# Two-layer hybrid decoder on one core: first operands, memory rows, row maxima and last output rearranged

## The chip, the core and the metric

The kernel runs on one core of one Trainium2 chip. The metric is device time in microseconds of one execution. A core has a matrix engine (TensorE, PE in the profile; its weight loads are listed as PEld), a vector engine (DVE), a scalar engine (ACT), GpSimd (POOL), and SyncE (SP), which here only issues transfers. Each engine works through its own instructions in order, and semaphores tie them together.

## What is computed

A residual stream of 256 rows by 1024 columns goes through two layers and a last normalisation. Cut to what matters here:

```python
def hybrid_layer(x, mem, ...):
    h = rms_norm(x, g_mix)
    z = h @ w_in                      # q, k, v of 6 + 6 heads, q of 4 heads, 3 gate blocks
    gates = sigmoid(z[..., o3:])
    o_a = dilated_mixer(...)          # 6 heads, masked softmax, three groups mixed
    o_b = moba_attn(...)              # 6 heads, causal softmax
    o_m = memory_attn(q_m, rms_norm(mem, g_mem), w_mkv)   # 4 heads on 256 memory rows
    y = gates[0] * (o_a @ w_pa) + gates[1] * (o_b @ w_pb) + gates[2] * (o_m @ w_pm)
    x = x + y @ w_o
    hm = rms_norm(x, g_mlp)
    return x + square(relu(hm @ w_up)) @ w_down

for l in range(2):
    x = hybrid_layer(x, mem, ...)
out = rms_norm(x, norm_final)
```

## The kernel before

Every product is made in two-part precision. A float32 matrix is split into a rounded part `hi` and the rest `lo`; a product is then hi·hi + hi·lo + lo·hi, three matmuls (`mm3`). The weights, 1 MB or 768 KB at a time (a *unit*), are brought in by SP into one of three `raw` buffers. ACT copies a rounded `whi` from it and DVE subtracts to get `wlo` (`split_to`, lines 139 and 140). Activations are transposed by PE, multiplied by the gain, and split the same way into `ax` (`split_gain`, lines 163 and 164).

A unit is used in two to four *groups*. The last loop of the kernel runs over the groups and sets the order on all engines: for group j come first the small matmuls hung on it (`pe`, `mid`), then the group's own products (`emit`), the work in `pre`, then `split_to(j + 3)`, the next transfers, the work in `post`, and last the copying out of the group's own sums. `whi` and `wlo` have five buffers, so the splits can run ahead of the products by some groups. PSUM has eight banks, given out in the order in which they were freed (`ps`, `pf`).

Groups 0 to 5 of layer 1 make one block of gates, in pieces of one and two k-tiles, while x and the weights arrive tile by tile. Ahead of them PE runs 15 transposes of the identity (`WARM`), which nobody reads. Both k-tiles of a pair are transposed into one PSUM bank, ACT then takes `hi` and DVE `lo` of one k-tile after the other (`first_pair`). Groups 6 to 17 make q, k and v of six heads. Their rotary part is done by DVE (lines 235, 236) and GpSimd (237, 238).

The memory rows are brought into a fourth use of the `raw` buffers at group 14, squared and summed by ACT at groups 17 and 18 (`mem_stats`, line 208), and their projection for k and v, `w_mkv`, is used in groups 24 to 27.

The scores of a head are made at the start of its group (`h_scores`). `h_max` (line 361) then adds the mask, takes the row maximum and frees the bank. It stands in `post`, behind the split of a later group's weights. Exponentials (391), sums and scaling (416), transposes (424) and the product with v follow in later groups.

At the end the last group adds 256 columns at a time to x for the second 128 rows, squares them on ACT, multiplies by the last gain, and scales by the power -0.5 of the mean square that GpSimd takes (`finish_out`). The output leaves in four transfers from SP.

Of the kernel before, what the change touches and what calls it, by code (L numbers as in the profile page):

```python
# [11 lines left out]
F32 = mybir.dt.float32  # L12
F32R = mybir.dt.float32r
BF16 = mybir.dt.bfloat16
AF = mybir.ActivationFunctionType
ALU = mybir.AluOpType
# [3 lines left out]
P = 128  # L20
D = 1024
S = 256
# [11 lines left out]
SHUF = list(range(8, 16)) + list(range(0, 8)) + list(range(16, 32))  # L34
QK_SCALE = HD ** -0.5
LOOK = 3
WARM = 15


@with_exitstack  # L40
def hybrid_kernel(ctx, tc, x, mem, memT, gains, g_final, rope, masks, w_in, w_pa, w_pb, w_pm,
                  w_out, w_mkv, w_up, w_down, out):
    nc = tc.nc
# [9 lines left out]
    def ps():  # L53
        b = free_banks.popleft()
        t = psp.tile([P, 512], F32, tag=f"b{b}", name=f"ps_b{b}", bufs=1)
        bank_of[id(t)] = (b, t)
        return t

    def pf(t):
        free_banks.append(bank_of.pop(id(t))[0])  # L60

    def sb(shape, dt, tag, bufs, shift=None):

        n = int(np.prod(shape[1:]))
# [27 lines left out]
    gain = sb([P, 3 * DEPTH, KT], F32, "gain", 1)  # L95
    xs = sb([P, 2, D], F32, "x", 1)
# [65 lines left out]
    def split_gain(hi, lo, src, g):  # L162
        nc.scalar.activation(hi, src, AF.Copy, scale=g)
        nc.vector.scalar_tensor_tensor(lo, src, g, f32(hi), op0=ALU.mult, op1=ALU.subtract)
# [40 lines left out]
    def square_sum(src, acc, keep=True):  # L205
        w = src.shape[1]
        junk = sb([P, 1024], BF16, "P", 5)[:, :w] if keep else src
        nc.scalar.activation(junk, src, AF.Square, accum_out=acc)
# [275 lines left out]
    def layer(l):  # L484
# [10 lines left out]
        for n in range(2):  # L495
            for br in range(3):
                col = OG + br * D + n * 512
                b = {}

                def emit(first, last, ks, br=br, n=n, b=b):  # L500
                    def f(hi, lo):
                        if first:
                            b["p"] = [ps() for _ in range(2)]
                        for t in range(2):
                            tt = slice(t * P, (t + 1) * P)
                            for c, k in enumerate(ks):
                                ah, al, _ = st["hT"][k // 4]
                                mm3(b["p"][t], ah[:, k % 4, tt], al[:, k % 4, tt], hi[:, c, :],
                                    lo[:, c, :], k == 0, k == KT - 1)
                        if last:  # L510
                            fn = AF.Copy if b["raw"] else AF.Sigmoid

                            def ev():
                                for t in range(2):
                                    nc.scalar.activation(
                                        gate(br, t, n), b["p"][t], fn,
                                        scale=1.0 if b["raw"] else st["rstd"][:, t:t + 1])
                                    pf(b["p"][t])
                            return ev
                    return f  # L520

                def block(emit=emit, col=col, cuts=((2, 2), (2, 2))):
                    for h, cut in enumerate(cuts):
                        k0 = 4 * h
                        ks = [k0 + sum(cut[:i]) for i in range(len(cut))]
                        unit([(win[:, k0:k0 + 4, col:col + 512], 4)], 4, 512, cut,
                             [emit(k == 0, k + c == KT, list(range(k, k + c)))
                              for k, c in zip(ks, cut)])
                b["raw"] = len(gate_units) < n_raw
                if b["raw"]:  # L530
                    raw_blocks.append((br, n))
                gate_units.append(block)
# [291 lines left out]
        add = lambda g, w, fn, i, *a: groups[g][w].append(lambda: fn(l, i, *a))  # L824
        for i in range(16):
            add(S0[i], "pe", h_scores, i)
            add(S0[i], "post", h_max, i)
            if i in (2, 5):
                add(S0[i] + 1, "post", h_exp, i - 2, i)
                d = 0 if l and i == 2 else 1  # L830
                add(S0[i] + 1 + d, "post", h_exp, i - 1, i)
                add(S0[i] + 2 + d, "post", h_exp, i, i)
                add(S0[i] + 3 + d, "pre", h_den, i)
                dens.update({ii: S0[i] + 3 + d for ii in range(i - 2, i + 1)})
            elif i >= 6:
                add(S0[i] + 1, "post", h_exp, i, i)
                add(S0[i] + 2, "pre", h_den, i)
                dens[i] = S0[i] + 2
# [75 lines left out]
    def finish_out(t, acc=None, r2=None):  # L914

        m0, o0 = fin[t]
        o1 = sb([P, 512], F32, "P", 5)
        r = sb([P, 1], F32, "fr", 2)
        pieces = [rs_state[DEPTH - 1, "next"][:, t, 1:2]]
        if acc is not None:  # L920
            s2 = sb([P, 2], F32, "ss2", 1)
            pieces = [s2[:, i:i + 1] for i in range(2)]
            for i in range(2):
                xx = xs[:, t, 512 + 256 * i:768 + 256 * i]
                nc.vector.scalar_tensor_tensor(xx, acc[t, 1][:, 256 * i:256 * i + 256],
                                               r2[:, t:t + 1], xx, op0=ALU.mult, op1=ALU.add)
                square_sum(xx, pieces[i])
        nc.vector.tensor_tensor(o1, xs[:, t, 512:], gfin[0][:, 512:], op=ALU.mult)
        for ss in pieces:
            ms = sb([P, 1], F32, "fm", 3)  # L930
            nc.vector.scalar_tensor_tensor(ms, ss, 1.0 / D, m0, op0=ALU.mult, op1=ALU.add)
            m0 = ms
        nc.gpsimd.tensor_tensor(r, ms, neghalf[:, 0:1], op=ALU.pow)
        if t == 0:
            nc.gpsimd.tensor_scalar(o1, o1, r, 1.0, op0=ALU.mult, op1=ALU.mult)
        else:
            nc.vector.tensor_scalar(o1, o1, r, None, op0=ALU.mult)
        nc.sync.dma_start(out[t * P:(t + 1) * P, 512:], o1)
        nc.scalar.activation(o0, o0, AF.Copy, scale=r)
        nc.sync.dma_start(out[t * P:(t + 1) * P, :512], o0)  # L940
# [2 lines left out]
    mem_state = {}  # L943

    def mem_rows_load():
        mem_state["m"] = sb([P, 2, D], F32, "raw", 3)
        nc.sync.dma_start(mem_state["m"], mem.rearrange("(t p) d -> p t d", p=P))

    def mem_stats(t):
        if t == 0:  # L950
            mem_state["ss"] = sb([P, 2], F32, "ss0", 2)
        square_sum(mem_state["m"][:, t, :], mem_state["ss"][:, t:t + 1], keep=False)
# [69 lines left out]
    first_ps = {}  # L1022

    def first_transpose(c):
        p = first_ps[c] = ps()
        for i in range(4):
            k, t = 2 * c + i // 2, i % 2
            nc.tensor.transpose(p[:, i * P:(i + 1) * P], xs[:, t, k * P:(k + 1) * P], ident)

    def first_operand(k):  # L1030
        hi, lo, _ = L[0]["hT"][k // 4]
        p = first_ps[k // 2]
        split_gain(hi[:, k % 4, :], lo[:, k % 4, :], p[:, k % 2 * S:(k % 2 + 1) * S],
                   gain[:, 0, k:k + 1])
        if k % 2:
            pf(p)

    def first_pair(c):
        first_transpose(c)
        first_operand(2 * c)  # L1040
        first_operand(2 * c + 1)


    busy = ps()
    for _ in range(WARM):
        nc.tensor.transpose(busy[:, :P], ident, ident)
    pf(busy)
    warm = sb([P, 2], F32, "warm", 1)
    nc.scalar.activation(warm, neghalf, AF.Exp)
    first_transpose(0)  # L1050
    for k in range(2):
        first_operand(k)
        split_to(k)

    def first_stats():
        ss = sb([P, 2], F32, "ss0", 2)
# [1 line left out]
            square_sum(xs[:, t, :], ss[:, t:t + 1])  # L1058
        L[0]["rstd"] = rstd_of(mean_square(ss, 1), "rstd")

    for c, j in ((1, 0), (2, 2), (3, 3)):
        groups[j]["pre"].append(lambda c=c: first_pair(c))
    groups[5]["pre"].append(first_stats)
    groups[8]["mid"] = lambda: row_tables(0, L[0]["rstd"])
    g1, gm = L[1]["g0"], [L[l]["g_mem"] for l in range(DEPTH)]
    groups[gm[0] - 10]["pre"].append(mem_rows_load)
    groups[gm[0] - 7]["post"].append(lambda: mem_stats(0))
    groups[gm[0] - 6]["post"].append(lambda: mem_stats(1))
    groups[gm[0] - 4]["pre"].append(mem_rstd)
    groups[gm[0] + 1]["mid"] = mem_rows  # L1070
    for l in range(DEPTH):
# [88 lines left out]
```

## Time and profile before

| | |
|---|---|
| runs, median (lowest to highest) | 770.65 us (770.24 to 771.03), 3 runs |
| the profiled execution | 771.88 us, its span 770.1 us |
| PE busy | 755.7 us |
| DVE busy | 569.1 us |
| ACT busy | 466.8 us |
| GpSimd busy | 73.9 us |
| read from memory | 137.52 MB, 180 GB/s over the span |

A row of the timeline gives start, duration, engine, line, operation, output <- inputs with their shapes, and in brackets how long the engine had stood idle before it and what released it. Consecutive matmuls overlap, so the time that one costs is the distance from its start to the next one's start, not its listed duration. In a row of waits the numbers are the total, how often, and the longest.

### The profile page before, as it was taken

What the parts mean: (1) busy time and instruction counts of PE and PEld (TensorE: products, weight loads), DVE (VectorE), ACT (ScalarE), POOL (GpSimd) and SP (SyncE); (2) the same over time, 40 slices, a digit from 0 to 9 for tenths busy, and PEclk for the clock granted to TensorE, in tenths of its full rate; (3) what the DMA queues carried; (4) which work ended last, traced back from release to release, by engine and by line L of the source; (5) the groups of instructions that cost most, each with busy time, mean ns of one, the idle gap of its engine ahead of it and who ended that gap; (6) DMA issues with size and microseconds to landing.
All of it is one profiled execution on the core that took longest, in us unless ns stands there. A gap on an engine that the chain in (4) does not pass through costs nothing.

```text
span 770.1 us, 11176 instructions
## 1 busy us (share of the span) xinstructions
PE 755.7 (98%) x4237; PEld 663.6 (86%) x4237; DVE 569.1 (74%) x969; ACT 466.8 (61%) x812; POOL 73.9 (10%) x79
## 2 busy tenths in 40 slices
PE   8999999999999999999999999999999999999996
PEld 6998899888888888898889899888888888888885
DVE  4799999849786655766568989986787766566654
ACT  4777878784565544655455777869546555445542
POOL 1342030003000000000003211300110000000000
PEclk9999999999999999999999999999999999999999
DMA  8847444544647558565536455453655655666441
GB/s 280 254 158 260 126 168 159 166 163 165 196 139 244 165 186 273 183 199 165 205 123 201 154 183 172 151 181 125 203 172 165 200 191 164 203 219 206 163 151 54
DMA packets 92197, 139.28 MB, mean 181 GB/s; under 512 B 2928, under 2 KB 53104, under 8 KB 92144
## 3 DMA queue, kind: packets, MB, share of 16 engines
q1 hardware_dynamic: 92000, 138.55, 54.7%
q8 instruction: 33, 0.54, 0.3%
q14 instruction: 20, 0.16, 0.1%
q10 hardware_dynamic: 144, 0.02, 0.0%
HBM read 137.52 MB, written 1.05 MB: 180 GB/s over the span
## 4 chain that ended last, share of the span: by engine, by line
PE 57%; issue 29%; DVE 7%; ACT 4%; POOL 2%; DMA 1%; POOLq 0%; ACTq 0%; DVEq 0%
PE ps_b L148 13%; PE ps_b L149 13%; PE ps_b L150 13%; PE ps_b L154 8%; PE ps_b L155 4%; DVE wlo L140 2%; PE ps_b L424 1%; ACT whi L139 1%; DVE qk L218 1%; PE ps_b L451 1%; POOL rs L237 1%; PE ps_b L344 1%; POOL rc L238 1%; PE ps_b L343 1%; PE ps_b L450 1%
## 5 line engine op out<-in xcount | busy, mean ns | idle before, releaser
L140 DVE TENSOR_TENSOR wlo<-raw,whi 128x1024 fp32r<-128x1024 f32 (+2 forms) x266 | 305.7, 1180 | 46.3 <-ACT whi L139 45.7
L139 ACT ACTIVATE whi<-raw 128x1024 fp32r<-128x1024 f32 (+2 forms) x266 | 260.2, 1008 | 28.5 <-PE ps_b L150 9.7
L154 PE MATMUL ps_b<-ax,whi 128*128 128x512 f32 x512 | 179.5, 391 | 0.0
L155 PE MATMUL ps_b<-ax,wlo 128*128 128x256 f32 x512 | 144.3, 282 | 0.0
L148 PE MATMUL ps_b<-whi,ax 128*128 128x512 f32 (+1 forms) x320 | 125.6, 393 | 1.8 <-ACT whi L139 1.8
L149 PE MATMUL ps_b<-wlo,ax 128*128 128x512 f32 (+1 forms) x320 | 122.1, 381 | 0.2 <-DVE wlo L140 0.2
L150 PE MATMUL ps_b<-whi,ax 128*128 128x512 f32 (+1 forms) x320 | 122.0, 381 | 0.0
L154 PEld LDWEIGHTS ps_b<-ax,whi 128*128 128x128 f32 x512 | 96.1, 188 | 20.6
L148 PE MATMUL ps_b<-whi,qk 128*128 128x512 f32 x256 | 99.8, 390 | 0.0
L149 PE MATMUL ps_b<-wlo,qk 128*128 128x512 f32 x256 | 99.8, 390 | 0.0
L150 PE MATMUL ps_b<-whi,qk 128*128 128x512 f32 x256 | 99.7, 389 | 0.0
L155 PEld LDWEIGHTS ps_b<-ax,wlo 128*128 128x128 f32 x512 | 96.7, 189 | 1.1
L703 ACT ACTIVATE P<-ps_b 128x256 f32<-128x256 f32 x64 | 24.1, 382 | 104.8 <-PE ps_b L155 104.8
L705 DVE TENSOR_TENSOR P<-ps_b,P 128x256 f32<-128x256 f32 x64 | 26.7, 423 | 76.1 <-ACT P L703 76.1
L148 PEld LDWEIGHTS ps_b<-whi,ax 128*128 128x128 f32 x320 | 60.4, 189 | 11.1 <-ACT whi L139 2.6
L150 PEld LDWEIGHTS ps_b<-whi,ax 128*128 128x128 f32 x320 | 60.3, 189 | 10.4
L149 PEld LDWEIGHTS ps_b<-wlo,ax 128*128 128x128 f32 x320 | 60.5, 189 | 9.6 <-DVE wlo L140 1.0
L148 PE MATMUL ps_b<-ax,whi 128*128 128x256 f32 x224 | 63.6, 284 | 0.0
L149 PE MATMUL ps_b<-ax,whi 128*128 128x256 f32 x224 | 62.7, 280 | 0.0
L150 PE MATMUL ps_b<-ax,wlo 128*128 128x256 f32 x224 | 62.7, 280 | 0.0
L148 PEld LDWEIGHTS ps_b<-whi,qk 128*128 128x128 f32 x256 | 48.1, 188 | 10.1
L150 PEld LDWEIGHTS ps_b<-whi,qk 128*128 128x128 f32 x256 | 48.1, 188 | 10.1
(150 smaller groups left out, 1076.4 us busy)
## 6 DMA issues: line engine op xcount, KB each, us to landing
raw<-in_w_up SPq DMA_DIRECT2D x32, 1024.0 KB, 5.9
raw<-in_w_down SPq DMA_DIRECT2D x32, 1024.0 KB, 4.9
raw<-in_w_in SPq DMA_DIRECT2D x24, 1024.0 KB, 5.1
raw<-in_w_in SPq DMA_DIRECT2D x24, 768.0 KB, 4.5
raw<-in_w_out SPq DMA_DIRECT2D x8, 1024.0 KB, 5.0
raw<-in_w_mkv SPq DMA_DIRECT2D x4, 1024.0 KB, 5.2
raw<-in_w_pm SPq DMA_DIRECT2D x4, 512.0 KB, 3.3
raw<-in_w_pb SPq DMA_DIRECT2D x4, 512.0 KB, 3.7
```

Of the source, the lines that this page charges most:

```text
L139: nc.scalar.activation(hi, src, AF.Copy)
L140: nc.vector.tensor_sub(lo, src, f32(hi))
L148: nc.tensor.matmul(o, lhsT=lh, rhs=rh, start=start, stop=False)
L149: nc.tensor.matmul(o, lhsT=lh, rhs=rl, start=False, stop=False)
L150: nc.tensor.matmul(o, lhsT=ll, rhs=rh, start=False, stop=stop)
L154: nc.tensor.matmul(o, lhsT=lh, rhs=rr, start=start, stop=False)
L155: nc.tensor.matmul(o[:, :S], lhsT=ll, rhs=rr[:, 0, :], start=False, stop=stop)
L218: nc.vector.tensor_sub(q[b, j, :], qf[a, :], f32(q[a, j, :]))
L237: nc.gpsimd.tensor_tensor(sh, sh, sinr, op=ALU.mult)
L238: nc.gpsimd.tensor_tensor(c, c, sh, op=ALU.add)
L703: nc.scalar.activation(tt[:, i, :], p[i][:, S:], AF.Copy)
L705: nc.vector.tensor_tensor(tt[:, i, :], p[i][:, :S], tt[:, i, :], op=ALU.add)
```

## The change

- **First operands.** The idle transposes are 12 ahead of the first pair of x tiles and 4 behind it, in place of 15 ahead. Each k-tile is transposed into a bank of its own. The first k-tile gets `hi` and `lo` both from DVE, and ACT begins with the first two splits of weights. The second pair is taken k-tile by k-tile, each followed by its split of weights. In groups of one k-tile the three terms run hi·hi, lo·hi, hi·lo, each over both row halves.
- **Memory rows.** They are loaded at group 8, in place of 14, into the buffer that later holds the gates (`gate12`), not into a `raw` buffer. Their squares move to groups 11 and 12.
- **Masks and row maxima.** `h_max` moves from `post` to `pre`, ahead of its group's `split_to`, for all 16 heads of both layers.
- **Last output.** For the second 128 rows the multiplication by the gain is cut in two, half of it behind the mean; the scaling is shared by ACT (256 columns) and DVE; ACT issues one of three transfers. The two squares share one scratch buffer.

```diff
-WARM = 15
+WARM = (12, 4)
...
+                    def f1(hi, lo):
...
+                        for a, w in ((ah, hi), (al, hi), (ah, lo)):
+                            for t in range(2):
+                                nc.tensor.matmul(b["p"][t], lhsT=a[:, k % 4, t * P:(t + 1) * P],
+                                                 rhs=w[:, 0, :], start=first and a is ah and w is hi,
+                                                 stop=False)
...
-            add(S0[i], "post", h_max, i)
+            add(S0[i], "pre", h_max, i)
...
+            junk = sb([P, 1024], BF16, "P", 5)
             for i in range(2):
...
-                square_sum(xx, pieces[i])
+                nc.scalar.activation(junk[:, 256 * i:256 * i + 256], xx, AF.Square,
+                                     accum_out=pieces[i])
+            m = sb([P, 1], F32, "fm", 3)
+            nc.vector.tensor_tensor(o1[:, :256], xs[:, t, 512:768], gfin[0][:, 512:768],
+                                    op=ALU.mult)
+            nc.vector.scalar_tensor_tensor(m, pieces[0], 1.0 / D, m0, op0=ALU.mult, op1=ALU.add)
+            ms = sb([P, 1], F32, "fm", 3)
+            nc.vector.scalar_tensor_tensor(ms, pieces[1], 1.0 / D, m, op0=ALU.mult, op1=ALU.add)
+            r = sb([P, 1], F32, "fr", 2)
+            nc.gpsimd.tensor_tensor(r, ms, neghalf[:, 0:1], op=ALU.pow)
+            nc.vector.tensor_tensor(o1[:, 256:], xs[:, t, 768:], gfin[0][:, 768:], op=ALU.mult)
+            nc.scalar.activation(o0[:, 256:], o0[:, 256:], AF.Copy, scale=r)
+            nc.scalar.dma_start(out[t * P:(t + 1) * P, 256:512], o0[:, 256:])
+            nc.vector.tensor_scalar(o1, o1, r, None, op0=ALU.mult)
+            nc.sync.dma_start(out[t * P:(t + 1) * P, 512:], o1)
+            nc.vector.tensor_scalar(o0[:, :256], o0[:, :256], r, None, op0=ALU.mult)
+            nc.sync.dma_start(out[t * P:(t + 1) * P, :256], o0[:, :256])
+            return
...
-        mem_state["m"] = sb([P, 2, D], F32, "raw", 3)
+        mem_state["m"] = sb([P, 4096], F32, "gate12", 1)[:, :2 * D].rearrange(
+            "p (t d) -> p t d", t=2)
...
-        p = first_ps[c] = ps()
-        for i in range(4):
-            k, t = 2 * c + i // 2, i % 2
-            nc.tensor.transpose(p[:, i * P:(i + 1) * P], xs[:, t, k * P:(k + 1) * P], ident)
+        for k in (2 * c, 2 * c + 1):
+            p = first_ps[k] = ps()
+            for t in range(2):
+                nc.tensor.transpose(p[:, t * P:(t + 1) * P], xs[:, t, k * P:(k + 1) * P], ident)
...
+            nc.vector.tensor_scalar(hi[:, 0, :], p[:, :S], g, None, op0=ALU.mult)
+            nc.vector.scalar_tensor_tensor(lo[:, 0, :], p[:, :S], g, f32(hi[:, 0, :]),
+                                           op0=ALU.mult, op1=ALU.subtract)
...
+    keep_busy(WARM[0])
...
     first_transpose(0)
-    for k in range(2):
-        first_operand(k)
-        split_to(k)
+    keep_busy(WARM[1])
+    pf(busy)
+    first_operand(0)
+    split_to(0)
+    split_to(1)
+    first_operand(1)
...
+    groups[0]["pre"].append(second_pair)
...
-    groups[gm[0] - 10]["pre"].append(mem_rows_load)
-    groups[gm[0] - 7]["post"].append(lambda: mem_stats(0))
-    groups[gm[0] - 6]["post"].append(lambda: mem_stats(1))
+    groups[gm[0] - 16]["pre"].append(mem_rows_load)
+    groups[gm[0] - 13]["post"].append(lambda: mem_stats(0))
+    groups[gm[0] - 12]["post"].append(lambda: mem_stats(1))
```

ACT at the start of the program, before the change. `ax` is the activation operand, `whi` the rounded weights, a number behind a name tells buffers apart:

```order
L1049 ACT_TABLE_LOAD
L1049 ACTIVATE warm<-neghalf 128x2
L163 ACTIVATE ax<-ps_b_131,gain 128x256
L139 ACTIVATE whi<-raw 128x512
L163 ACTIVATE ax<-ps_b_131,gain 128x256
L139 ACTIVATE whi<-raw 128x512
L163 ACTIVATE ax<-ps_b_156,gain 128x256 x2
L139 ACTIVATE whi<-raw 128x512 x2
```

The same place after the change:

```order
L1081 ACT_TABLE_LOAD
L1081 ACTIVATE warm_126<-neghalf_67 128x2
L139 ACTIVATE whi_140<-raw_92 128x512
L139 ACTIVATE whi_144<-raw_92 128x512
L163 ACTIVATE ax_111<-ps_b2_131,gain_88 128x256
L163 ACTIVATE ax_111<-ps_b5_158,gain_88 128x256
L139 ACTIVATE whi_166<-raw_92 128x512
L163 ACTIVATE ax_111<-ps_b6_161,gain_88 128x256
L139 ACTIVATE whi_172<-raw_92 128x512
```

Two splits of weights now stand ahead of the first operand that ACT takes, and every operand comes out of a bank of its own.

DVE at group 24, before the change, from the scaling of the first head's exponentials (416) to the copying out of the second rotary tile (235, 236); `ps_b7_863` are the scores of the fourth head:

```order
L416 TENSOR_SCALAR P_679<-P_679,rd_896 128x128
L416 TENSOR_SCALAR P_679<-P_679,rd_896 128x256
L140 TENSOR_TENSOR wlo_901<-raw_762,whi_900 128x1024
L361 ISA P_907,mxt_906<-ps_b7_863,mask_91 128x128
L361 ISA mxt_906 128x1
L361 ISA P_907,mxt_906<-ps_b7_863,mask_91 128x256
L361 ISA mxt_906 128x1
L235 TENSOR_TENSOR rc_910<-cosr_319,ps_b3_734 128x256
L236 STREAM_SHUFFLE rs_911<-ps_b3_734 128x256
```

The same place after the change:

```order
L361 ISA P_904,mxt_903<-ps_b5_868,mask_91 128x128
L361 ISA mxt_903 128x1
L361 ISA P_904,mxt_903<-ps_b5_868,mask_91 128x256
L361 ISA mxt_903 128x1
L416 TENSOR_SCALAR P_679<-P_679,rd_901 128x128
L416 TENSOR_SCALAR P_679<-P_679,rd_901 128x256
L140 TENSOR_TENSOR wlo_910<-raw_774,whi_909 128x1024
L235 TENSOR_TENSOR rc_915<-cosr_324,ps_b4_739 128x256
L236 STREAM_SHUFFLE rs_916<-ps_b4_739 128x256
```

The row maximum (361) has gone ahead of the scaling and of the split; the nine instructions are the same nine, and the rotary tile still ends the row.

## Rows read from the trace of the kernel before

**Rows 1.** Page, part 1: busy time, share of span, instructions per engine.

```profile
PE 755.7 (98%) x4237; PEld 663.6 (86%) x4237; DVE 569.1 (74%) x969; ACT 466.8 (61%) x812; POOL 73.9 (10%) x79
```

**Rows 2.** Waits of PE, whole span: total us, times, longest.

```profile
PE ps_b L424 <- DVE P L416: 1.4, 1, 1.4
...
PE ps_b L424 <- DVE mxt L361: 0.8, 1, 0.8
PE ps_b L150 <- DVE wlo L140: 0.7, 1, 0.7
```

**Rows 3.** Timeline, first 23 us: start, duration, engine, line, operation, idle before.

```profile
1.38 3.46 PE L1046 MATMUL ps_b<-ident 128*128 128x128 f32 x15 [1.38 <-POOL ident masks.py:199]
...
4.64 1.06 PE L1028 MATMUL ps_b<-ident,x 128*128 128x128 f32 x4
...
6.10 0.62 ACT L139 ACTIVATE whi<-raw 128x512 fp32r<-128x512 f32 x1
6.24 0.48 DVE L164 SCALAR_TENSOR_TENSOR ax<-ps_b,gain,ax 128x256 fp32r<-128x256 f32 x1 [6.24 <-ACT ax L163]
...
6.75 0.69 DVE L140 TENSOR_TENSOR wlo<-raw,whi 128x512 fp32r<-128x512 f32 x1
...
6.78 0.80 PE L148 MATMUL ps_b<-whi,ax 128*128 128x512 f32 x1 [1.08 <-ACT whi L139]
...
8.94 0.63 PE L149 MATMUL ps_b<-wlo,ax 128*128 128x512 f32 x1
...
9.37 0.63 PE L150 MATMUL ps_b<-whi,ax 128*128 128x512 f32 x1
...
12.77 0.49 PE L148 MATMUL ps_b<-whi,ax 128*128 128x512 f32 x1 [0.72 <-ACT whi L139]
...
22.53 0.28 PE L148 MATMUL ps_b<-ax,whi 128*128 128x256 f32 x1
```

**Rows 4.** Stretches: length, busy us of each engine, granted clock, DMA share, GB/s.

```profile
5.00:10.00 5.00, 3.92 (x11) 2.49 (x10) 2.20 (x4) 1.98 (x4) 0.00 (x0) 1.00 0.98 332
```

**Rows 5.** Transfers issued in the first 1.4 us: count, size, us to landing.

```profile
x<-in_x SPq DMA_DIRECT2D x1, 256.0 KB, 3.4
raw<-in_w_in SPq DMA_DIRECT2D x1, 256.0 KB, 3.5
```

**Rows 6.** Timeline of ACT, then of DVE, 30 to 75 us.

```profile
34.03 0.86 ACT L216 ACTIVATE qk<-rc 64x256 fp32r<-64x256 f32 x2 [1.68 <-POOL rc L238]
...
55.72 1.06 ACT L208 ACTIVATE raw<-raw 128x1024 f32<-128x1024 f32 x1
...
54.66 1.14 DVE L313 SCALAR_TENSOR_TENSOR Va<-ps_b,rstd,Va 128x384 fp32r<-128x384 f32 x2 [0.63 <-ACT Va L312]
...
58.02 0.96 DVE L140 TENSOR_TENSOR wlo<-raw,whi 128x768 fp32r<-128x768 f32 x1 [0.24 <-ACT whi L139]
...
73.30 0.43 DVE L236 STREAM_SHUFFLE rs<-ps_b 128x256 f32<-128x256 f32 x1
```

**Rows 7.** Timeline of DVE and PE in layer 2, at its first scores.

```profile
435.17 1.23 DVE L140 TENSOR_TENSOR wlo<-raw,whi 128x1024 fp32r<-128x1024 f32 x1 [0.28 <-ACT whi L139]
...
436.52 0.42 DVE L361 CUSTOM_DVE_ANT_0 P<-ps_b,mask 128x256 f32<-128x256 f32 x1
...
437.24 0.39 PE L148 MATMUL ps_b<-whi,ax 128*128 128x512 f32 x1
437.47 0.39 PE L149 MATMUL ps_b<-wlo,ax 128*128 128x512 f32 x1
```

**Rows 8.** Timeline of the end, from the last gain to the last transfer.

```profile
764.28 0.69 DVE L928 TENSOR_TENSOR P<-x,gate 128x512 f32<-128x512 f32 x1 [0.24 <-ACT P L208]
...
765.40 0.56 POOL L933 TENSOR_TENSOR fr<-fm,neghalf 128x1 f32<-128x1 f32 x1 [1.77 <-DVE fm L931]
765.99 0.72 ACT L939 ACTIVATE P<-P,fr 128x512 f32<-128x512 f32 x1 [1.35 <-POOL fr L933]
...
766.88 0.43 SPq L940 DMA_DIRECT2D out<-P  x1
```

More of the change, by code (lines that the diff above doesn't have):

```diff
@@ L500, in emit, with f0 @@
                 def emit(first, last, ks, br=br, n=n, b=b):
-                    def f(hi, lo):
+                    def f0(hi, lo):
                         if first:
@@ L509, in f, with f2 @@
                                     lo[:, c, :], k == 0, k == KT - 1)
+                    def f1(hi, lo):
+                        k = ks[0]
+                        if first:
+                            b["p"] = [ps() for _ in range(2)]
+                        ah, al, _ = st["hT"][k // 4]
+                        for a, w in ((ah, hi), (al, hi), (ah, lo)):
[3 more added lines that the diff above has]
+                                                 stop=False)
+                    def f2(hi, lo):
+                        f0(hi, lo)
                         if last:
@@ L519, in f @@
                             return ev
-                    return f
+                    return f1 if len(ks) == 1 else f2
                 def block(emit=emit, col=col, cuts=((2, 2), (2, 2))):
@@ L917, in finish_out @@
         o1 = sb([P, 512], F32, "P", 5)
-        r = sb([P, 1], F32, "fr", 2)
         pieces = [rs_state[DEPTH - 1, "next"][:, t, 1:2]]
@@ L926, in finish_out @@
                                                r2[:, t:t + 1], xx, op0=ALU.mult, op1=ALU.add)
-                square_sum(xx, pieces[i])
+                nc.scalar.activation(junk[:, 256 * i:256 * i + 256], xx, AF.Square,
[16 more added lines that the diff above has]
+            return
+        r = sb([P, 1], F32, "fr", 2)
         nc.vector.tensor_tensor(o1, xs[:, t, 512:], gfin[0][:, 512:], op=ALU.mult)
[L929 to L932, printed above, removed]
+        ms = sb([P, 1], F32, "fm", 3)
+        nc.vector.scalar_tensor_tensor(ms, pieces[0], 1.0 / D, m0, op0=ALU.mult, op1=ALU.add)
         nc.gpsimd.tensor_tensor(r, ms, neghalf[:, 0:1], op=ALU.pow)
[L934 to L937, printed above, removed]
+        nc.gpsimd.tensor_scalar(o1, o1, r, 1.0, op0=ALU.mult, op1=ALU.mult)
         nc.sync.dma_start(out[t * P:(t + 1) * P, 512:], o1)
@@ L1024, in first_transpose, with keep_busy @@
     def first_transpose(c):
-        p = first_ps[c] = ps()
-        for i in range(4):
-            k, t = 2 * c + i // 2, i % 2
-            nc.tensor.transpose(p[:, i * P:(i + 1) * P], xs[:, t, k * P:(k + 1) * P], ident)
+        for k in (2 * c, 2 * c + 1):
+            p = first_ps[k] = ps()
+            for t in range(2):
+                nc.tensor.transpose(p[:, t * P:(t + 1) * P], xs[:, t, k * P:(k + 1) * P], ident)
     def first_operand(k):
         hi, lo, _ = L[0]["hT"][k // 4]
[L1032 to L1041, printed above, removed]
+        p = first_ps[k]
+        if k:
+            split_gain(hi[:, k % 4, :], lo[:, k % 4, :], p[:, :S], gain[:, 0, k:k + 1])
+        else:
+            g = gain[:, 0, :1]
+            nc.vector.tensor_scalar(hi[:, 0, :], p[:, :S], g, None, op0=ALU.mult)
+            nc.vector.scalar_tensor_tensor(lo[:, 0, :], p[:, :S], g, f32(hi[:, 0, :]),
+                                           op0=ALU.mult, op1=ALU.subtract)
+        pf(p)
     busy = ps()
-    for _ in range(WARM):
-        nc.tensor.transpose(busy[:, :P], ident, ident)
-    pf(busy)
+    def keep_busy(count):
+        for _ in range(count):
+            nc.tensor.transpose(busy[:, :P], ident, ident)
+    keep_busy(WARM[0])
     warm = sb([P, 2], F32, "warm", 1)
@@ L1059, in first_stats, with second_pair, next_pair @@
         L[0]["rstd"] = rstd_of(mean_square(ss, 1), "rstd")
-    for c, j in ((1, 0), (2, 2), (3, 3)):
-        groups[j]["pre"].append(lambda c=c: first_pair(c))
+    def second_pair():
+        first_transpose(1)
+        for k in (2, 3):
+            first_operand(k)
+            split_to(k)
+    def next_pair(c):
+        first_transpose(c)
+        for k in (2 * c, 2 * c + 1):
+            first_operand(k)
+    groups[0]["pre"].append(second_pair)
+    for c, j in ((2, 2), (3, 3)):
+        groups[j]["pre"].append(lambda c=c: next_pair(c))
     groups[5]["pre"].append(first_stats)
```

## The prediction

> **What bounds the kernel now.** I read the page's busy shares first: PE is busy 755.7 us, 98% of the span [rows 1]. So almost everything is matmul time that this change leaves alone, and only three things can move the end: the stretches in which PE stands, the stretch in which it runs slowly, and what comes after its last product. Next I read the waits of PE [rows 2]. They are few: 0.7, 0.8 and 1.4 us, all on DVE and all between 60 and 90 us, in layer 1's attention. The third view is the timeline of the first 23 us [rows 3]. There PE stands 1.08 us ahead of its first real product at 6.78, and 0.72 us again at 12.77. It also runs slowly: products of 512 columns start 0.43 us apart at 8.94 and 9.37, the 1.2 GHz level, where later they start 0.23 apart, the 2.4 GHz level [rows 7]. The granted clock of 5 to 10 us is printed as 1.00 [rows 4]; the distances contradict it there, and I go by them. The same row shows the DMA engines 0.98 busy, so the first tiles arrive as fast as they can. The last view is the end: the chain from the last gain through GpSimd's power to the last output transfer [rows 8].
>
> **First operands.** Before, 15 idle transposes and then the pair's own four run from 1.38; the 15 take 4.64 - 1.38, or 0.217 us each [rows 3]. Twelve end at 3.99. The first x transfer lands 3.4 us after an issue inside the first microsecond [rows 5], so at about 4.1, and the pair starts at about 4.15. Four transposes are 0.87 us, to 5.02, and four more idle ones end at 5.89. Is the first product ready by then? From the start of a lone transpose to its reader is 1.06 us for four [rows 3], less three distances of 0.217, or 0.41. So DVE can begin on the first k-tile at 4.15 + 0.22 + 0.41 = 4.78. The new `hi` on DVE is an instruction that the trace of before does not show. Its nearest row is `lo` at 0.48 us on the same shape, which also reads a second tensor; I take 0.48, between a half of it and all of it. Then `hi` is there at 5.26, `lo` at 5.74, and `wlo` (0.69) at 6.43. ACT, whose first tile of weights lands at about 4.7 (3.5 us after an issue at about 1.2, [rows 5]), has `whi` (0.62) at 5.4. So all is ready and PE starts at 5.9 in place of 6.78.
>
> From there I count PE's own work up to the first product of the q block, which before starts at 22.53 [rows 3]. It is 48 products (six in each of four groups, twelve in each of two) at 0.227, or 10.9 us, and three sets of four transposes at about 0.35, together 11.9 us at the high clock. Now the clock. Before, PE was still slow at 9.37 [rows 3]; I put the rise right behind that, at 10.0, and take the same moment for the change. Work done between 5.9 and 10.0 runs at half speed, which costs 4.1 / 2 = 2.05 us. The end is 5.9 + 11.9 + 2.05 = 19.9, against 22.53: a gain of 2.6 us.
>
> This holds only if no operand is late. Before, ACT took its second `hi` of a pair only when DVE had read its `lo` of the first out of the same bank; with a bank for each k-tile it need not wait. Group 0 ends at 5.9 + 6 x 0.43 = 8.5, the second pair's transposes at 9.35, ACT has `hi` and `whi` of k-tile 2 at about 10.6, DVE its `wlo` at 11.3. PE comes to them at 11.1 and needs `wlo` only at its fifth product, at 12.0. So the wait of 0.72 goes, and what is next late is nothing up to the q block. If instead the old waits came back whole, 0.72 and about 0.5 behind it, the gain would be 1.4. If the clock rose before the first product, PE would be bound by the arriving weights. The last two tiles' splits then make the end about 18.3, a gain of 4.2. These are the ends, 1.4 and 4.2.
>
> Does the gain last? The weights' splits behind it run five groups ahead and wait for PE to free buffers, so they move with it; the transfers wait on the splits and have DMA time over. DVE's own chain starts from sums that PE gives it in the q block, so it moves too.
>
> **Memory rows.** ACT's two squares (1.06 us, [rows 6]) stand now in a stretch in which ACT has no pause. DVE waits behind them: 0.63 us for the copies of v and 0.24 us for a split [rows 6], some 0.9 together, and I add 0.3 for smaller pauses. At groups 11 and 12 ACT has pauses, 1.68 us in one row, while it waits for GpSimd's rotary part [rows 6], so there I cost the squares at nothing; without that cover each costs its 1.06 us on ACT, of which DVE would feel a part. The load at group 8 is queued on SP between two weight units and needs no free `raw` buffer, so nothing behind it waits for a buffer. It lengthens the next unit's landing by some 3 us (1 MB at the 332 GB/s of [rows 4]), which the run ahead of several groups hides. The `raw` buffer that it gives back lets the units of `w_mkv` start sooner.
>
> What does PE get from it? Its last wait, 1.4 us, ends when DVE has scaled the third head [rows 2]. Up to that instruction DVE has the same work as before, so PE's release moves by exactly the pauses that DVE loses: 1.2 us. The waits do not vanish. I expect some 1.9 of the 2.9 us to stay. The bounds are 0.3 (only the short pause goes) and 2.9 (all go).
>
> **Masks and row maxima.** The same instructions in another order: the 0.8 us wait at the first transposes of probabilities is for the bank that `h_max` frees [rows 2], and that now comes sooner. But right behind it PE needs the bank that the rotary copy at 73.30 frees [rows 6], and in both orders that comes after the same nine instructions. The wait moves by one instruction of PE and keeps its end, so the gain is nothing. The cost: what `h_max` is moved past, `wlo` of a group three further on, comes later by its 0.6 to 0.7 us (0.42 of it in [rows 7]). The tightest place I found is layer 2's first scores. There `wlo` ends at 436.40 and PE reads it at 437.47 [rows 7], 1.07 us of room; 0.28 of the addition falls into a pause of DVE. I take nothing. The bounds are a gain of 0.8 (the bank was the end) and a loss of 0.6 at each of the six earliest heads of the two layers, 3.6.
>
> **Last output.** Before, DVE's gain product of 0.69 us at 764.28 stands ahead of the mean, which waits for nothing else; GpSimd starts at 765.40 [rows 8]. Now half of it stands ahead and half behind, and GpSimd can start once the second square is in, at about 764.95: 0.45 us. Behind the power, ACT's scaling of 512 columns (0.72) ended ahead of the last issue at 766.88 [rows 8]; now 256 columns on DVE behind a scaling of 512 give the last issue at about 766.4, so 0.5 in all. The last piece is half as large, which gives up to 0.3 more. I take 0.7, between 0.3 and 0.9. On the second queue, the Trainium skill ("Trainium Kernel Development and Optimization", Key Constraints) says that queues of several engines share the same 16 DMA engines and save issue time alone. By that the term would be 0.5; no row of before has output on two queues.
>
> **Sum.** 2.6 + 1.2 + 0 + 0.7 = 4.5 us. The profiled execution took 771.88 us, a span of 770.1 and 1.8 around it; the sum makes that 767.4. The median of the runs, 770.65, is 1.2 lower than the profiled one, and I carry the gain over to it: 766.1.
>
> **The rivals.** *The clock rises sooner (0.28).* PE now never stands between 1.38 and the first products but for some 0.2 us, where it stood 1.08 us before. If the idle transposes keep the clock's count going, PE is at 2.4 GHz by the first groups, and the head gains 4.2: 770.65 - 4.2 - 1.2 - 0.7 = 764.5. Against it stands that the 19 transposes up to 4.64 + 1.06 = 5.7 left the products at 9.37 slow. The Trainium skill ("TensorE: Matmul & The Clock Gate", Part 4) says that transposes do not count as busy for the clock. By that this rival falls, and the forecast stands; the rows at 8.94 and 9.37 agree but cannot prove it, since PE also stood in between.
>
> *The head's gain is eaten (0.12).* DVE's pauses in this stretch are short [rows 6]. If it is the bound from its first split on, and its chain does not start sooner, PE reaches the same three waits 2.6 us earlier and waits that much longer: 770.65 - 1.2 - 0.7 = 768.7. Against it stands that DVE's chain begins with PE's sums.
>
> *The maxima hold up the splits (0.05), slower.* In `pre`, DVE waits for PE's scores ahead of each split. If the run ahead were lost at every head, each of 32 would cost 0.6 us or more: 19 us, less the 4.5, makes 785. It is slower than before from some 8 heads on. Only layer 1's first heads and those of [rows 7] have so little room.
>
> *Nothing moves (0.05)*: 770.6, where the transfers set the head after all, and DVE the rest.
>
> **How the numbers follow.** The forecast has 0.50, and its own range is 764.9 to 767.5 from the bounds of its terms. About 0.2% (1.5 us) is what a measurement of this kernel can tell from no change. Faster by more: the forecast, the sooner clock and most of the third case, 0.90; within it 0.06; slower 0.04. The range from 763.8 to 768.7 takes in the sooner clock and the eaten gain, and leaves out some 0.15.
>
> **What would show it.** Right: the first product at 5.9, no wait of PE between there and the q block, which starts near 19.9; the 1.08 and 0.72 gone; waits of PE between 60 and 90 us of 1.5 to 2.2 us, with the 0.7 on `wlo` gone; no squares on ACT near 52; the last power about 0.45 us closer to the last product. Wrong: products 0.23 apart before 8 us (the sooner clock), waits of PE in that stretch of 4 us or more (the eaten gain), or new waits on `wlo` at the groups of scores (the slower rival).

## The result and the profile after

The changed kernel takes 765.17 us (median of 5 runs, 764.85 to 765.66) against 770.65 us (770.24 to 772.18) for the kernel before: a ratio of 0.9925, 95% interval 0.9911 to 0.994. It is 5.5 us faster, where 4.5 was forecast. The profiled execution took 765.22 us, a span of 763.4. The span has lost 6.7 us, more than the median, because the profiled execution of before was 1.2 us above its own median; what those 1.2 us were turns out to matter below.

Part 1 of the page of the changed kernel, in the columns of [rows 1]:

```profile
PE 753.7 (99%) x4238; PEld 663.5 (87%) x4238; DVE 568.1 (74%) x972; ACT 465.1 (61%) x811; POOL 70.7 (9%) x79
```

Its waits of PE, in the columns of [rows 2]:

```profile
PE ps_b L1077 <- POOL ident masks.py:199: 1.4, 1, 1.4
PE ps_b L344 <- DVE kz L229: 0.9, 1, 0.9
PE ps_b L424 <- DVE P L416: 0.5, 1, 0.5
PE ps_b L1057 <- DMA x<-in_x: 0.2, 1, 0.2
```

The first line is the wait for the identity at the start, the second the one at layer 2's first scores. Neither is touched: the kernel before has both, at the same length, and the prediction's list of the waits left the second one out. Between 60 and 90 us 0.5 is left of the 0.7, 0.8 and 1.4 of [rows 2]. The forecast left 1.9.

The start of the timeline, to be held against [rows 3]:

```profile
1.38 2.82 PE L1077 MATMUL ps_b<-ident 128*128 128x128 f32 x12 [1.38 <-POOL ident masks.py:199]
4.37 1.12 PE L1057 MATMUL ps_b<-ident,x 128*128 128x128 f32 x4 [0.16 <-DMA x<-in_x]
5.09 0.48 DVE L1067 TENSOR_SCALAR ax<-ps_b,gain 128x256 fp32r<-128x256 f32 x1 [5.09 <-PE ps_b L1057]
5.27 1.06 PE L1077 MATMUL ps_b<-ident 128*128 128x128 f32 x4
5.99 1.75 PE L519 MATMUL ps_b<-whi,ax 128*128 128x512 f32 x4
7.57 0.63 PE L519 MATMUL ps_b<-wlo,ax 128*128 128x512 f32 x2
8.39 1.17 PE L519 MATMUL ps_b<-whi,ax 128*128 128x512 f32 x4
...
18.96 0.28 PE L148 MATMUL ps_b<-ax,whi 128*128 128x256 f32 x1
```

The first product starts at 5.99 (forecast 5.9), and the new `hi` on DVE costs the 0.48 us that the forecast took. But from 7.57 on two products start 0.23 us apart: PE is at its 2.4 GHz level by then, where the forecast put the rise at 10.0. The trace agrees: its records of the granted clock begin at 7.22 us, and in the kernel before at 10.33. Ahead of its first record a view prints 1.00, and so [rows 4] shows 1.00 for a stretch in which PE was slow. The q block starts at 18.96, 3.6 us sooner than in [rows 3], where 19.9 was forecast. That is the rival with the sooner clock. From there to the last product the changed kernel gains 2.9 us more, and behind it 0.2.

The end, to be held against [rows 8]:

```profile
756.68 0.88 DVE L940 SCALAR_TENSOR_TENSOR x<-ps_b,r,x 128x256 f32<-128x256 f32 x2 [0.96 <-PE ps_b L150]
758.27 0.42 DVE L952 TENSOR_TENSOR P<-x,gate 128x256 f32<-128x256 f32 x1
758.44 0.67 POOL L951 TENSOR_TENSOR fr<-fm,neghalf 128x1 f32<-128x1 f32 x1 [1.29 <-DVE fm L949]
759.14 0.51 ACT L953 ACTIVATE P<-P,fr 128x256 f32<-128x256 f32 x1 [0.98 <-POOL fr L951]
...
760.03 0.43 SPq L958 DMA_DIRECT2D out<-P  x1
```

From the last addition to x to the power it is 1.76 us, and before it was 765.40 - 763.16 = 2.24: the 0.48 forecast as 0.45. The rest of that term did not come (point 4 below).

### The profile page after: what moved, and what is told of

It is laid out like the page before. It is cut to its first block, busy times and chain, and to the rows that moved or that the text cites. A ratio compares the mean times of both kernels' runs of the same rounds, so it can differ in the third digit from the quotient of the medians.

```text
span 763.4 us, 11175 instructions
## 1 busy us (share of the span) xinstructions
PE 753.7 (99%) x4238; PEld 663.5 (87%) x4238; DVE 568.1 (74%) x972; ACT 465.1 (61%) x811; POOL 70.7 (9%) x79
## 4 chain that ended last, share of the span: by engine, by line
PE 56%; issue 30%; DVE 7%; DMA 2%; POOL 2%; ACT 2%; SPq 0%; POOLq 0%; DVEq 0%; ACTq 0%
PE ps_b L148 13%; PE ps_b L150 13%; PE ps_b L149 13%; PE ps_b L154 8%; PE ps_b L155 4%; DVE wlo L140 2%; DMA raw<-in_w_in 2%; PE ps_b L424 1%; DVE qk L218 1%; PE ps_b L451 1%; PE ps_b L344 1%; PE ps_b L343 1%; PE ps_b L450 1%; POOL rs L237 1%; POOL rc L238 1%
## 5 line engine op out<-in xcount | busy, mean ns | idle before, releaser
L148 PE MATMUL ps_b<-whi,ax 128*128 128x512 f32 (+1 forms) x312 | 121.6, 390 | 0.0
L150 PE MATMUL ps_b<-whi,ax 128*128 128x512 f32 (+1 forms) x312 | 118.4, 379 | 0.0
L149 PE MATMUL ps_b<-wlo,ax 128*128 128x512 f32 (+1 forms) x312 | 118.2, 379 | 0.0
L150 PEld LDWEIGHTS ps_b<-whi,ax 128*128 128x128 f32 x312 | 58.6, 188 | 10.1
L149 PEld LDWEIGHTS ps_b<-wlo,ax 128*128 128x128 f32 x312 | 58.8, 188 | 8.4
L148 PEld LDWEIGHTS ps_b<-whi,ax 128*128 128x128 f32 x312 | 58.7, 188 | 8.2
```

The source lines that it names most:

```text
L148: nc.tensor.matmul(o, lhsT=lh, rhs=rh, start=start, stop=False)
L149: nc.tensor.matmul(o, lhsT=lh, rhs=rl, start=False, stop=False)
L150: nc.tensor.matmul(o, lhsT=ll, rhs=rh, start=False, stop=stop)
```

## The experiments

**The old kernel again, and each part alone on it.** Three kernels that differ from the old one by one part each, with the old one beside them. These edits are pieces of the diff shown above; the line that stands for each is given.

The old kernel once more (no edit):

> The kernel before once more, unchanged, to see how fixed its first 23 us are. If the moment at which TensorE's clock rises is set by the program, products are again 0.43 us apart at 9.4 us, the q block starts at 22.5 and the time is 770.6. If the moment is chance, the first products 0.23 apart come elsewhere, and the start of the q block moves by half of that shift, up to 1.5 us, and the time with it.

Measured: 770.59 us, ratio 1.0 [0.9992, 1.0009]. Its 12 runs spread from 768.97 to 772.14. The products are 0.43 us apart at 9.4 us and the q block starts at 22.50, as in the first profile.

The first operands alone:

```diff
-WARM = 15
+WARM = (12, 4)
```

> The kernel before with the first operands alone. My forecast's head term says 2.6 us (768.0). The sooner clock says 3.6 as in the changed kernel's trace, the q block at 19.0 (767.0). The eaten gain says under 0.5 us (770.2 or more), with the waits of PE between 60 and 90 us longer by what the head gained. If the parts help each other in the middle, those waits stay near the 3.1 us of before.

Measured: 767.83 us, ratio 0.9965 [0.9953, 0.9977], 2.7 us faster. Its q block starts at 18.39, 4.1 sooner, so by the median some 1.4 of the head's gain is lost again behind it. The waits of PE between 60 and 90 us are 2.9 us.

The memory rows alone:

```diff
-    groups[gm[0] - 10]["pre"].append(mem_rows_load)
+    groups[gm[0] - 16]["pre"].append(mem_rows_load)
```

> The kernel before with the memory rows alone. My term says 1.2 us (769.4), with waits of PE between 60 and 90 us of about 1.9 in place of 3.1. If the memory rows alone carry the whole middle, 2.6 to 2.9 us (767.9) and waits of about 0.5.

Measured: 770.03 us against 770.5, ratio 0.9997 [0.9988, 1.0005]: no gain that can be told. The waits between 60 and 90 us are 2.4 us, where the kernel before has 3.1 in its first profile and 2.2 in its second.

The masks and row maxima alone:

```diff
-            add(S0[i], "post", h_max, i)
+            add(S0[i], "pre", h_max, i)
```

> The kernel before with masks and row maxima alone ahead of the splits. My term says nothing (770.6 within 0.3): the wait at the first transposes of probabilities goes, the next one takes its length. If the order is worth something by itself (GpSimd's rotary steps beside other DVE instructions, or the bank), 0.8 to 1.5 us (769.5). If it holds up the splits, slower by 0.5 to 3 us, with waits of PE on wlo.

Measured: 769.58 us, ratio 0.9987 [0.9978, 0.9997], 0.9 us faster, where the prediction has nothing. The 0.8 us wait for the bank of the maxima is gone, the one right behind it has grown from 0.2 to 0.5, and the 1.4 us wait has become 0.6.

Memory rows and masks together:

```diff
+    groups[gm[0] - 16]["pre"].append(mem_rows_load)
...
+            add(S0[i], "pre", h_max, i)
```

> The kernel before with the memory rows and the masks, no change at the head or the end. If the two terms just add, their sum of 1.2 us (769.4) by my prediction. If together they free PE's middle, as in the changed kernel's trace, 2.5 to 2.9 us (767.9), with waits of about 0.5 between 60 and 90 us. If it takes the earlier start of DVE from the head as well, clearly less than 2.5.

Measured: 769.25 us, ratio 0.998 [0.9971, 0.9989], 1.2 us faster, with waits of 1.0 us there.

Added up, the head, the masks and the memory rows alone make 2.7 + 0.9 + 0.5 = 4.1 us, and the whole change makes 5.5. The last output adds little to this (below), so at least two parts seem to be worth more together. The next runs take one part out of the changed kernel each; again one or two lines stand for each edit.

**One part taken out.** The last output as before:

```diff
-            nc.scalar.dma_start(out[t * P:(t + 1) * P, 256:512], o0[:, 256:])
-            nc.vector.tensor_scalar(o1, o1, r, None, op0=ALU.mult)
```

> The changed kernel with the old last output. My term says 0.7 us slower than the changed one (765.9). The changed kernel's trace, from the last product to the end of the span, says 0.2 (765.4).

Measured: 765.43 us (765.05 to 765.55). The part is worth some 0.2 us. The runs alone could not tell that from nothing, but the traces say the same: from the last additions to x to the end of the span it is 6.93 us here and 6.75 in the changed kernel.

The memory rows as before:

```diff
-    groups[gm[0] - 16]["pre"].append(mem_rows_load)
+    groups[gm[0] - 10]["pre"].append(mem_rows_load)
```

> The changed kernel with the memory rows loaded and squared where they were before (group 14, a raw buffer; groups 17 and 18). Alone on the old kernel this part gained 0.1 to 0.5 us, on top of the masks 0.3. If the parts add up: 765.6, with PE waits between 60 and 90 us of 0.8 to 1.0. If the part is worth more once the head's gain brings PE 3.6 us earlier to the same chain of DVE (the whole gained 5.3, the parts alone some 4.3): 766.2 to 766.5, with waits of 1.5 us or more there.

Measured: 767.11 us (766.81 to 767.82). The part is worth 1.9 us here, against 0.5 or less alone, and PE waits 1.6 us between 60 and 90. This is where the parts do not add up.

The masks and maxima as before:

```diff
-            add(S0[i], "pre", h_max, i)
+            add(S0[i], "post", h_max, i)
```

> The changed kernel with the masks and row maxima behind the split of weights again, as before. The prediction costs this part at nothing: 765.3. Alone on the old kernel it gained 0.9; if the parts add up: 766.2, with the 0.8 us wait for the bank of the row maxima back. If it is this part that is worth more once PE comes earlier: 766.7 to 767.2, and waits between 60 and 90 us of 2 us or more.

Measured: 766.2 us (766.02 to 766.46). The part is worth 1.0 us here and 0.9 alone: it adds up.

The changed kernel again, beside the last two:

> The changed kernel once more, beside the three others on the same chip: 765.3, within 0.4. Its profile tells whether the 2.4 GHz level, which came at 7.5 us in the first, comes at the same moment: with the level there by 7.5 us or sooner the q block starts at 18.2 to 19.0.

Measured: 765.23 us (765.16 to 765.33), the q block at 18.67.

**What the four idle transposes do.** Without them in the changed kernel, and with four more on the old one:

```diff
-WARM = (12, 4)
+WARM = (12, 0)
```

> The changed kernel without the four idle transposes behind the first pair, so that PE stands from about 5.3 until the first operands are there at 5.9. If the fill is what brings the clock up at 7 us, products are 0.43 apart until about 10 and the q block starts near 20 (766.2). If the clock rises without it, nothing changes (765.2). If the fill only delays the first product, up to 0.2 us faster.

```diff
     first_transpose(0)
+    busy = ps()
+    for _ in range(4):
+        nc.tensor.transpose(busy[:, :P], ident, ident)
+    pf(busy)
```

> The kernel before with four idle transposes behind the first pair and nothing else. If filling the pause brings the clock up sooner, products are 0.23 apart from about 7 us, though the operands still come as before; the gain is then small, 0 to 1 us (770.0), since PE waits for operands at 12.8 anyway. If transposes do not count for the clock, it rises near 10 as before (770.6).

Measured: without them 765.42 us, no slower by the median, but the six runs go from 764.58 to 767.01, where the changed kernel stays within 0.8. With four more on the old kernel 770.6 us, ratio 0.9994 [0.9985, 1.0003]. So the transposes alone do not make the head's gain. They do go with an early rise: in the profiled execution of the old kernel with four more, 769.68 us, products are 0.23 us apart from 7.84 on and the q block starts at 21.20 in place of 22.53. The median does not show these 1.3 us; where they go is open. Here is PE in the profiled execution without them, which took 766.72 us:

```profile
4.24 1.11 PE L1057 MATMUL ps_b<-ident,x 128*128 128x128 f32 x4
5.59 2.05 PE L519 MATMUL ps_b<-whi,ax 128*128 128x512 f32 x4 [0.24 <-ACT whi L139]
7.44 1.05 PE L519 MATMUL ps_b<-wlo,ax 128*128 128x512 f32 x2
```

Here is the old head in the kernel with memory rows and masks moved, whose profiled execution took 768.59 us:

```profile
4.64 1.06 PE L1029 MATMUL ps_b<-ident,x 128*128 128x128 f32 x4
6.78 0.49 PE L148 MATMUL ps_b<-whi,ax 128*128 128x512 f32 x1 [1.08 <-ACT whi L139]
```

In the first the products are 0.43 us and more apart until about 10.8. In the second, with the old head unchanged, the first product is already a fast one (0.49 long, against 0.80 in [rows 3]) and the q block starts at 21.2 in place of 22.5. The moment at which the clock rises is not set by the instructions alone: it differs between executions that issue the same ones. By the first record of the granted clock it came at 10.15 to 10.57 us in four of the six profiles with the old head, at 5.62 in the one just shown, and at 7.03 in the one with four more transposes; in the changed kernel without the four it came at 10.78. So it is there by 7.22 in all eight profiles with the four transposes, of the new head and of the old, and in one of the six without them. What they seem to buy is that the early case comes every time; with so few profiles that is a count and not a proof.

**A faster version.** The longest wait of PE that is left behind the start is 0.9 us at layer 2's first scores, on the rounded k. Scores of the first three groups there one group later:

```diff
-        S0 = [va, va + 1, va + 2, first - 2, first - 1, first]
+        S0 = [va + l, va + l + 1, va + l + 2, first - 2, first - 1, first]
```

> The changed kernel, with layer 2's first three groups of scores made one group later. In the changed kernel PE stands 0.9 us at layer 2's first scores (421.1 us), for the rounded k that DVE makes. If that wait ends with DVE's place in the order, one group later it is gone and nothing else is late there: 764.4, 0.9 faster than the changed kernel, and no wait on k in the list. Rival: what hangs behind the scores (exponentials, sums, transposes) is now late in turn, and the wait comes back as one on probabilities: 765.2 to 765.6, no faster.

Measured: 764.39 us (764.22 to 765.49), ratio to the kernel before 0.9917 [0.9901, 0.9932], and 0.8 us under the changed kernel beside it. One of its four runs, at 765.49, lies above all five of the changed kernel, so the gain rests on the other three and on the trace. All waits of PE that its profile lists:

```profile
PE ps_b L1077 <- POOL ident masks.py:199: 1.4, 1, 1.4
PE ps_b L424 <- DVE P L416: 0.6, 1, 0.6
```

The wait is gone and has not come back on probabilities.

## Why the prediction was right, and where its steps were not

The sign and the size of the gain hold. But masks and last output were mis-sized, the 1.2 of the memory rows lies between what they gave alone and inside, and the head's term fits only by an offset. The rival's 764.5 is even nearer to the measured 765.2 than the forecast's 766.1.

**1. First operands: 2.6 forecast, 2.7 alone, 3.8 inside.** The two agree for the wrong reason. The step that failed is the one that kept the clock's rise at 10.0. It is there by 7.2, and the q block starts 2.9 to 4.3 us sooner in the seven profiles with the whole new head, where the rival had 4.2. Alone, most of the difference is lost in the next 30 us, by the mechanism of point 2. The forecast knew neither.

The prediction named a rule of the Trainium skill against the early rise: "TensorE: Matmul & The Clock Gate", Part 4, has transposes not count as busy for the clock. The kernel with the head alone decides it. PE had run nothing but transposes here:

```profile
1.38 2.82 PE L1063 MATMUL ps_b<-ident 128*128 128x128 f32 x12 [1.38 <-POOL ident masks.py:199]
4.17 0.69 PE L1043 MATMUL ps_b<-ident,x 128*128 128x128 f32 x4
4.70 0.60 PE L1063 MATMUL ps_b<-ident 128*128 128x128 f32 x4
5.44 1.21 PE L519 MATMUL ps_b<-whi,ax 128*128 128x512 f32 x4
```

Four transposes from 4.17 take 0.53 us, 0.13 each, where those of [rows 3] were 0.217 apart, and the first products are 0.26 apart. The 2.4 GHz level came ahead of the first product; the first record of the granted clock is at 4.28. It is ahead of the first product in five of the fourteen profiles, one of them with the old head. In this kernel the rule does not hold, and the rival deserved more than 0.28.

**2. Memory rows: 1.2 forecast; 1.9 inside the change, 0 to 0.5 alone.** The forecast took its price from pauses of DVE in [rows 6], 0.63 us at the copies of v and 0.24 at a split. The second run of the same kernel has 0.25 at that split and no pause at the copies of v: the larger pause belongs to the execution, not to the kernel. In the profile of before, DVE's subtraction starts 0.07 us ahead of GpSimd's addition:

```profile
43.39 1.21 DVE L140 TENSOR_TENSOR wlo<-raw,whi 128x1024 fp32r<-128x1024 f32 x1
43.46 1.73 POOL L238 TENSOR_TENSOR rc<-rc,rs 128x256 f32<-128x256 f32 x1
45.23 0.42 ACT L227 ACTIVATE qk<-rc 64x256 fp32r<-64x256 f32 x1 [3.13 <-POOL rc L238]
```

In the second run of the same kernel a weight transfer landed late (at 42.5 us, and at 40.5 in the first), and the subtraction starts 0.20 us behind it:

```profile
43.46 0.74 POOL L238 TENSOR_TENSOR rc<-rc,rs 128x256 f32<-128x256 f32 x1
43.66 1.62 DVE L140 TENSOR_TENSOR wlo<-raw,whi 128x1024 fp32r<-128x1024 f32 x1 [0.17 <-ACT whi L139]
44.23 0.42 ACT L227 ACTIVATE qk<-rc 64x256 fp32r<-64x256 f32 x1 [0.20 <-POOL rc L238]
```

Whichever begins second is stretched: GpSimd's addition from 0.74 to 1.73, or the subtraction from 1.21 to 1.62. The Trainium skill ("SBUF — State Buffer", SBUF: two separate sides) says that GpSimd and a DVE instruction with two SBUF inputs hold a shared port in turn and the second one waits. These lengths agree to 0.15 us: the second one ends 0.59 and 1.08 us behind the first one's end, and it takes 0.74 and 1.21 undisturbed. When GpSimd begins second and so loses, ACT gets its input 1.0 us later. With the memory squares still ahead of ACT, it cannot catch up before DVE copies v. The distance from the sixth rotary tile, the last ahead of that copy, to the copy itself (L236 to L313) goes with it in all fourteen profiles. In the changed kernel with the old memory rows, and then in the changed kernel itself:

```profile
44.54 0.45 DVE L236 STREAM_SHUFFLE rs<-ps_b 128x256 f32<-128x256 f32 x1
...
51.60 1.14 DVE L313 SCALAR_TENSOR_TENSOR Va<-ps_b,rstd,Va 128x384 fp32r<-128x384 f32 x2 [0.63 <-ACT Va L312]
```

```profile
43.84 0.45 DVE L236 STREAM_SHUFFLE rs<-ps_b 128x256 f32<-128x256 f32 x1
...
49.96 1.14 DVE L313 SCALAR_TENSOR_TENSOR Va<-ps_b,rstd,Va 128x384 fp32r<-128x384 f32 x2
```

| L236 to L313 | GpSimd's addition 1.73 us | 0.74 us |
|---|---|---|
| squares at the old place | 7.06 in 3 profiles (before, head alone, old memory rows) | 5.97 in 3 (before again, masks alone, old head with four transposes) |
| squares at the new place | 6.11 to 6.13 in 5 (changed kernel twice, memory alone, memory and masks, no transposes) | 5.96 to 5.98 in 3 (old masks, old output, later scores) |

Moving the squares is worth 0.94 us if GpSimd loses and nothing if it wins. Both profiles with the new head and the old memory rows lose; the one old-kernel profile that loses is the one that took 1.2 us more than its median. That is the loss of point 1. Against the second run of before, which wins, the head alone is 4.1 us ahead at the q block, 3.5 at the copies of v and some 3 at the end of the span. Against the first run, which loses as it does, it is 4.1 ahead at the q block and 4.1 at the end. It is also a reason why head and memory rows are worth more together. No run forced the order of the two, and how often each falls in unprofiled runs is not shown.

The second half of the part's worth is in the weights behind it. With the old memory rows, `w_mkv` waits for the `raw` buffer that the squares hold: its first transfer is issued at 53.84, just as the second square ends, and in the changed kernel at 45.58. ACT and DVE wait behind it:

```profile
58.93 1.06 ACT L139 ACTIVATE whi<-raw 128x1024 fp32r<-128x1024 f32 x1 [0.87 <-DMA raw<-in_w_mkv]
...
64.48 1.23 DVE L140 TENSOR_TENSOR wlo<-raw,whi 128x1024 fp32r<-128x1024 f32 x1 [0.47 <-ACT whi L139]
```

The changed kernel has neither wait. The prediction named this gain and left it without a number. No run moved the squares without the load, so the two halves are told apart by the traces alone.

On the old head the part has a cost of its own. The step that fails is that the longer landing of the next unit is one "which the run ahead of several groups hides". The memory rows alone, ACT and DVE at groups 11 and 12:

```profile
33.75 0.85 ACT L139 ACTIVATE whi<-raw 128x768 fp32r<-128x768 f32 x1 [3.24 <-PE ps_b L150]
34.50 1.05 ACT L208 ACTIVATE gate<-gate 128x1024 f32<-128x1024 f32 x1
34.63 1.41 DVE L140 TENSOR_TENSOR wlo<-raw,whi 128x768 fp32r<-128x768 f32 x1 [1.62 <-ACT whi L139]
```

DVE pauses 1.62 us, and from the second to the third rotary tile it takes 4.72 us where the old place has 4.10. The trace puts ACT's wait to PE, but it ends with a transfer. This unit is issued at 27.13, behind the 1 MB of memory rows, and lands 6.5 us later, at 33.64, 0.1 us ahead of ACT; before, it is issued at 27.02 and lands in 4.4. The squares come behind this and no wait of DVE ends with them, so their cost of nothing stands. In the changed kernel the same distance is 4.10, and 4.35 in its second profile.

**3. Masks and row maxima: nothing forecast, 0.9 alone and 1.0 inside.** The step that failed is "the wait moves by one instruction of PE and keeps its end", since "in both orders that comes after the same nine instructions". They are the same nine, but they do not last as long. With the old masks, and then in the changed kernel, from the seventh rotary tile to the eighth:

```profile
63.72 0.45 DVE L236 STREAM_SHUFFLE rs<-ps_b 128x256 f32<-128x256 f32 x1
65.07 0.86 POOL L238 TENSOR_TENSOR rc<-rc,rs 128x256 f32<-128x256 f32 x1
65.26 1.75 DVE L140 TENSOR_TENSOR wlo<-raw,whi 128x1024 fp32r<-128x1024 f32 x1
67.83 0.43 DVE L236 STREAM_SHUFFLE rs<-ps_b 128x256 f32<-128x256 f32 x1
```

```profile
63.55 0.44 DVE L236 STREAM_SHUFFLE rs<-ps_b 128x256 f32<-128x256 f32 x1
64.88 0.74 POOL L238 TENSOR_TENSOR rc<-rc,rs 128x256 f32<-128x256 f32 x1
65.69 1.21 DVE L140 TENSOR_TENSOR wlo<-raw,whi 128x1024 fp32r<-128x1024 f32 x1
67.16 0.44 DVE L236 STREAM_SHUFFLE rs<-ps_b 128x256 f32<-128x256 f32 x1
```

The first takes 4.11 us, the second 3.61. The row maxima fill the time in which GpSimd works, and the subtraction starts as GpSimd ends. Between the first copies of v and the next, the seven subtractions of 1024 columns sum to 9.62 us with the old masks and 8.77 with the new. Not every one gains: the first and the third of the four behind the seventh tile are 0.54 us shorter, the second is 0.24 longer, since GpSimd's multiplication (237) now starts ahead of it. The four sum to 5.94 or 5.95 in all six profiles with the old masks and to 5.09 or 5.10 in all eight with the new. The three waits of PE in that stretch fall from 1.4 + 0.3 + 0.2 to 0.5. The loss feared in the prediction, splits that come too late at 32 heads, does not appear: no wait on `wlo` is in the list.

**4. Last output: 0.7 forecast, 0.2 measured.** The power moved as said. The term was mis-sized behind it. The last issue comes 0.37 us sooner against the last addition, and the step "half as large, which gives up to 0.3 more" has the wrong sign. Issues of the changed kernel's last 7 us, with size and us to landing:

```profile
out<-P SPq DMA_DIRECT2D x3, 256.0 KB, 2.3
out<-P ACTq DMA_DIRECT2D x1, 128.0 KB, 2.4
out<-P SPq DMA_DIRECT2D x1, 128.0 KB, 2.6
```

Before, four of 256 KB landed in 2.2 us each. From the last issue to the end it is 3.4 us, and it was 3.2. The rule of the Trainium skill that the prediction named ("Trainium Kernel Development and Optimization", Key Constraints) made the term 0.5, which was nearer.

**5. The sum.** Inside the change the parts are worth 1.9 (memory rows), 1.0 (masks) and 0.2 (last output), each as what the changed kernel loses without it. The head is the rest against memory and masks together: 769.25 - 765.2 - 0.2 = 3.8. These make 6.9, and the change 5.5: what head and memory rows only give together is counted with both. The forecast's 4.5 is near 5.5 because its errors had both signs, which is luck.

## What to carry to other kernels

Before a pause is made a term of a sum, see whether the profiled execution is itself above the median: its surplus may be that very pause, and a second profile of the same kernel tells. Where DVE subtracts two SBUF tensors while GpSimd works, look who starts first: another order of the same instructions made two such places half a microsecond shorter here, and a third one a quarter longer. Parts that feed the same chain are tried both alone and taken out of the whole, since here one of them was worth at most 0.5 alone and 1.9 inside.

## What the hardware showed that was not expected

- PE's rise to 2.4 GHz came at different moments in executions with the same instructions (at 10.15 to 10.57 us or at 5.62 with the old head), worth 1.3 us at the q block. The views print the granted clock as 1.00 in these stretches; the trace's first record of it gives the moment.
- Transposes alone were enough for it in five profiles, one of them with the old head.
- A weight transfer that held DVE's subtraction back by 0.27 us made ACT 1.0 us earlier, because GpSimd then began first.
- 128 KB of output took 2.6 us to land where 256 KB had taken 2.2.
